# A staging tile for the solve's transposed block, and three engines for the first diagonal copies of the inverse

## The chip, the cores and the metric

The kernel runs on one core of a Trainium2 chip. The metric is the device time of one execution in microseconds (us); lower is better. The kernel before took 1288.86 us as the median of three runs (1288.18 to 1288.86). The five engines are TensorE (PE in the profile), VectorE (DVE), ScalarE (ACT), GpSimd (POOL) and SyncE (SP), which here only issues transfers.

## What is computed

One layer of a two-branch encoder on a 2048 x 1024 float32 input: RMS norm, one input projection, a bidirectional gated delta rule over 4 heads of width 128, a windowed attention over 8 query heads, and one output projection added to the input. The part that matters here is the delta rule. For each head, direction and chunk it needs the inverse of a unit lower triangular matrix:

```python
m = jnp.where(strict, jnp.einsum('bhncd,bhnsd->bhncs', k_beta, k) * decay, 0.0)
t_inv = lax.linalg.triangular_solve(eye + m, jnp.broadcast_to(eye, m.shape),
                                    left_side=True, lower=True, unit_diagonal=True)
...
v_new = u_i - jnp.einsum('bhcd,bhde->bhce', w_i, state)
state = state * jnp.exp(g_last)[..., None, None] + jnp.einsum('bhcd,bhce->bhde', k_dec, v_new)
```

The state runs through all chunks of a head, forward and backward. A head's state steps can't begin before the first inverses of that head exist.

## The kernel before

Phase A (up to about 640 us) does the projections and the attention. Phase B works head by head, `h` = 0 to 3, with 16 chunks of 128 rows in each of two directions. For each head there are four stages:

- `pre_front(h)` loads the keys and queries (tile `kq`, from a ring of two buffers), values and decays four chunks at a time, four times over, and writes the matrices `ma` (line L704). It stores a copy of the key part in DRAM (`m_d`, L709).
- `solve(h)` inverts all 32 x 32 diagonal blocks of the head at once: 128 blocks, one on each partition. The 64 blocks of direction 0 have to be transposed within the partition. They are loaded into the lower half of tile `X` (L732), and DVE copies them, transposed, into `L` (L735). Then POOL clears all of `X` and writes ones on its diagonals (L736, L737). 31 pairs of DVE operations follow (L742 makes `tm`, L746 subtracts it from `X`), and the result goes to DRAM (`x_d`, L747).
- `invert(h)` builds the inverses of the 128 x 128 matrices from the blocks, in four rounds `hi` = 0 to 3. A round loads two groups of blocks (`xc`, L758), transposes them on DVE (`xt`, L759), and copies them onto the diagonals of three matrices `e1`, `e2`, `e3` (named `iv` in the trace; L764, L766, L768: 12 copies on POOL). Five products on PE follow (`pi`, L773), with ACT moving the results (L782 to L797). Each product waits for the one before it.
- `scan(h)` runs the 16 state steps of both directions. `py` (L822) is the matmul in which a step first uses the inverse. Round 0 of `invert` covers chunks 0 to 3 and 12 to 15, with which both directions begin, so the first step waits for round 0 alone.

The source calls `scan(h)`, `pre_front(h+1)`, `solve(h+1)` and `invert(h+1)` in that order, but this is not the order of execution. `set_order` plans the order of all instructions from a table of assumed costs and dependences and fixes it on each engine, so the stages of neighbouring heads overlap. The matmuls of one output projection (`pcs`, L600 to L602) are spread between as independent work. Each engine then works through its own list in order. A change in one place lets the planner lay out the whole program anew.

Of the kernel before, what the change touches and what calls it, by code (L numbers as in the profile page):

```python
# [7 lines left out]
F32 = mybir.dt.float32  # L8
F32R = mybir.dt.float32r
AF = mybir.ActivationFunctionType  # L10
# [5 lines left out]
P = 128  # L16
# [504 lines left out]
def phase_b(ctx, wide, late, tc, t, ident, consts, hp, mix_dn, mix_sw, kq_d, v_d, zdn_d, zsw_d, dp, out):  # L521
    nc = tc.nc
    V, A, G, T = nc.vector, nc.scalar, nc.gpsimd, nc.tensor
    dma = nc.sync.dma_start

    def pool(name, bufs=1, stack=ctx, **kw):
        return stack.enter_context(tc.tile_pool(name=name, bufs=bufs, reuse_waits="tile", **kw))
# [90 lines left out]
    q1 = pool("q1", stack=pre_stack)  # L618
# [6 lines left out]
    quads = [slice(32 * p, 32 * p + 32) for p in range(4)]  # L625
# [100 lines left out]
    def solve(h, H):  # L726
        m_d, x_d, _ = H["solve"]
        L = qa.tile([P, 32, 32], F32, tag="L", name=f"L{h}")
        X = qa.tile([P, 32, 32], F32, tag="X", name=f"X{h}")
        lv = [m_d[d].rearrange("u (p y) -> (u p) y", p=4)[:, : 32 * P] for d in range(2)]  # L730
        lv = [a.rearrange("q (r x) -> q r x", x=P)[:, :, :32] for a in lv]
        dma(X[0:64], lv[0])  # L732
        dma(L[64:128], lv[1])
        x = X.rearrange("p r c -> p (r c)")
        V.tensor_copy(L[0:64], X[0:64].rearrange("p r c -> p c r"))  # L735
        G.memset(x, 0.0)  # L736
        G.memset(x[:, ::33], 1.0)  # L737
        for c in range(31):
            n = 31 - c
            tm = qa.tile([P, 256], F32, tag="tm", name=f"tm{h}_{c}")  # L740
            tv = tm[:, : n * (c + 1)].rearrange("p (r k) -> p r k", k=c + 1)
            V.tensor_tensor(  # L742
                tv, L[:, c + 1 :, c : c + 1].to_broadcast([P, n, c + 1]),
                X[:, c : c + 1, 0 : c + 1].to_broadcast([P, n, c + 1]), ALU.mult,
            )
            V.tensor_tensor(X[:, c + 1 :, 0 : c + 1], X[:, c + 1 :, 0 : c + 1], tv, ALU.subtract)  # L746
        dma(x_d.rearrange("d u (p r) c -> (d u p) (r c)", p=4), X.rearrange("p r c -> p (r c)"))  # L747

    def invert(h, H):
        _, x_d, mp = H["solve"]  # L750
        for hi in range(4):
            e1, p2, e2, e3 = (z[hi % len(z)] for z in zts)
            m = mp[hi]
            x0, x1 = {}, {}
            for d, c4 in ((0, hi), (1, 3 - hi)):
                xc = qb.tile([P, 4, 32], F32, tag="xc", name=f"xc{h}_{d}_{c4}", bufs=4)
                xt = qb.tile([P, 4, 32], F32, tag="xt", name=f"xt{h}_{d}_{c4}", bufs=4)
                dma(xc, x_d[d, 4 * c4 : 4 * c4 + 4].rearrange("u i c -> i u c"))  # L758
                V.transpose(xt.rearrange("p u c -> p (u c)"), xc.rearrange("p u c -> p (u c)"))  # L759
                x0[d], x1[d] = (xc, xt) if d == 0 else (xt, xc)  # L760
            g = qb.tile([P, 4, P], F32, tag="g", name=f"g{h}_{hi}", bufs=2)
            G.tensor_tensor(g, m[:, :, 0], m[:, :, 1], ALU.add)
            for p, q in enumerate(quads):
                G.tensor_copy(e1[q, :, q], x0[p % 2][q])  # L764
            for p, q in enumerate(quads):
                G.tensor_copy(e2[q, :, q], x1[1 - p % 2][q])  # L766
            for p, q in enumerate(quads):
                G.tensor_copy(e3[q, :, q], x0[p // 2][q])  # L768

            def prod(j, lhs, rhs):  # L770
                o = ps_i[(hi + j) % 2].tile([P, 4, P], F32, tag="inv", name=f"pi{j}_{h}_{hi}")
                for c in range(4):
                    T.matmul(o[:, c], lhs(c), rhs(c), start=True, stop=True)  # L773
                return o

            def half(c):
                a = m[:, c].rearrange("p s i -> p (s i)")[:, :384].rearrange("p (e x) -> p e x", x=192)
                return a[:, :, :64]

            o = prod(0, lambda c: g[:, c], lambda c: e1[:, c])  # L780
            b1 = qb.tile([P, 4, P], F32, tag="b1", name=f"b1{h}_{hi}", bufs=2)
            A.activation(b1, o, AF.Copy, scale=-1.0)  # L782
            for d in range(2):
                for q in quads:
                    G.tensor_copy(m[q, :, 1 - d, q], x1[d][q])
            o = prod(1, lambda c: e2[:, c], lambda c: b1[:, c])
            for q, r in ((1, 0), (2, 3)):
                A.activation(e3[quads[q], :, quads[r]], o[quads[q], :, quads[r]], AF.Copy)
            o = prod(2, lambda c: b1[:, c], lambda c: e2[:, c])
            for r, q in ((0, 1), (1, 0), (2, 3), (3, 2)):  # L790
                A.activation(m[quads[r], :, 1 - r % 2, quads[q]], o[quads[r], :, quads[q]], AF.Copy)
            o = prod(3, lambda c: g[:, c], lambda c: e3[:, c])
            for d in range(2):
                A.activation(p2[halves[1 - d], :, halves[d]], o[halves[1 - d], :, halves[d]], AF.Copy, scale=-1.0)
            o = prod(4, lambda c: p2[:, c], half)
            for d in range(2):
                A.activation(m[halves[d], :, 1 - d, halves[1 - d]], o[halves[d], :, halves[1 - d]], AF.Copy)  # L797
# [93 lines left out]
    for f in late:  # L891
        f(zp)
    solve(0, H)
    zts = [[const(f"iv{j}_{i}", [P, 4, P], None, qb) for i in range(2 - j % 2)] for j in range(4)]
    for grp in zts:
        for a in grp:
            G.memset(a, 0.0)
    invert(0, H)
    wide.close()
    with tc.using_default_side("right"):  # L900
# [6 lines left out]
    for h in range(3):  # L907
        scan(h, H)
        H = pre_front(h + 1)
        solve(h + 1, H)  # L910
        invert(h + 1, H)
# [398 lines left out]
```

## Time and profile before

| | before |
|---|---|
| median of 3 runs | 1288.86 us |
| the profiled execution | 1286.12 us, its span 1284.2 us |
| mean granted PE clock in it | 0.993 |
| PE, DVE, ACT, POOL busy | 96%, 70%, 56%, 40% of the span |

The profile is of one execution. The 1.92 us between its time and its span lie outside the recorded instructions. The rows name the line, the engine, the operation and the tile written and read. A bracket at the end tells how long the engine had been idle before the row and what it waited for. A row can stand for several equal instructions (xN); its duration is then theirs together. Times are counted from the start of the span.

### The profile page before, as it was taken

How to read it: one execution, taken by the hardware profiler on the slowest of the kernel's cores; microseconds unless marked ns; L12 is line 12 of the kernel's file. 1: busy time of each engine (PE TensorE's matmuls, PEld its weight loads, DVE VectorE, ACT ScalarE, POOL GpSimd, SP SyncE). 2: the span in 40 equal slices, each digit the busy share in tenths (PEclk: the TensorE clock that was granted, in tenths of full speed). 3: DMA queues.
4: the chain of work that ended last, by engine and by line, in shares of the span. 5: the costliest groups of instructions: out<-in, count | busy, mean ns of one | idle time of the engine just before them, and what ended most of it. 6: DMA issues, size and time to landing. Idle time of an engine off the chain costs nothing.

```text
span 1284.2 us, 22568 instructions
## 1 busy us (share of the span) xinstructions
PE 1227.4 (96%) x7162; PEld 1056.0 (82%) x7162; DVE 901.8 (70%) x2266; ACT 718.8 (56%) x2121; POOL 507.8 (40%) x876
## 2 busy tenths in 40 slices
PE   6999999999999999999999998899799899999998
PEld 6998878788889987888888787788688789898776
DVE  4422488999874679999996583689489779557333
ACT  6421265776644677777665425858557855666210
POOL 2230054566512387774321306513681651641000
PEclk9999999999999999999999999999899999999999
DMA  7442254223544333421237816967965874746765
GB/s 259 150 127 79 97 169 158 88 83 101 177 130 131 121 106 111 124 98 50 75 115 242 237 63 196 283 192 206 278 172 157 242 202 139 207 148 201 242 233 210
DMA packets 225510, 205.35 MB, mean 160 GB/s; under 512 B 48496, under 2 KB 175088, under 8 KB 225392
## 3 DMA queue, kind: packets, MB, share of 16 engines
q1 hardware_dynamic: 225392, 203.92, 51.2%
q8 instruction: 57, 0.93, 0.3%
q14 instruction: 61, 0.50, 0.1%
HBM read 138.79 MB, written 65.08 MB: 159 GB/s over the span
## 4 chain that ended last, share of the span: by engine, by line
PE 67%; DVE 9%; DMA 9%; ACT 5%; POOL 4%; issue 4%; SPq 1%; DVEq 0%; POOLq 0%; ACTq 0%
PE pf_c L190 5%; PE pf_c L191 5%; PE pf_c L192 5%; PE pf_z L190 4%; PE pf_z L191 4%; PE pf_z L192 4%; PE pi L773 3%; PE pt L364 3%; PE pcd L562 2%; PE pcd L563 2%; PE pcd L564 2%; DVE acc L241 2%; PE pcs L601 2%; PE py L822 1%; PE pcs L600 1%
## 5 line engine op out<-in xcount | busy, mean ns | idle before, releaser
L190 PE MATMUL pf_c<-xhi,wh_c 128*128 128x512 f32 x384 | 151.3, 405 | 1.1 <-DVE acc L241 1.1
L191 PE MATMUL pf_c<-xlo,wh_c 128*128 128x512 f32 x384 | 152.0, 404 | 0.0
L192 PE MATMUL pf_c<-xhi,wl_c 128*128 128x512 f32 x384 | 150.6, 404 | 0.0
L241 DVE SCALAR_TENSOR_TENSOR acc<-pf_c,cw,acc 128x512 f32<-128x512 f32 (+1 forms) x192 | 140.4, 742 | 10.4 <-ACT acc L237 8.1
L359 POOL TENSOR_SCALAR pr<-pr,st 128x384 f32<-128x384 f32 (+1 forms) x128 | 88.8, 711 | 72.3 <-DVE st L357 56.5
L190 PE MATMUL pf_z<-xhi,wh_z 128*128 128x512 f32 x256 | 87.0, 403 | 0.5 <-DVE zo L214 0.5
L191 PE MATMUL pf_z<-xlo,wh_z 128*128 128x512 f32 x256 | 86.5, 399 | 0.0
L350 ACT ACTIVATE pr<-pr,st 128x384 f32<-128x384 f32 (+1 forms) x128 | 76.1, 597 | 17.7 <-DVE st L349 16.4
L192 PE MATMUL pf_z<-xhi,wl_z 128*128 128x512 f32 x256 | 85.3, 398 | 0.0
L190 PEld LDWEIGHTS pf_c<-xhi,wh_c 128*128 128x128 f32 x384 | 72.5, 189 | 14.8 <-DVE acc L241 1.5
L192 PEld LDWEIGHTS pf_c<-xhi,wl_c 128*128 128x128 f32 x384 | 72.2, 189 | 13.2
L191 PEld LDWEIGHTS pf_c<-xlo,wh_c 128*128 128x128 f32 x384 | 72.1, 189 | 13.1
L368 ACT ACTIVATE ph<-pt 128x512 fp32r<-128x512 f32 x92 | 53.8, 595 | 41.6 <-PE pt L364 38.2
L345 DVE CUSTOM_DVE_ANT_0 pr<-s,mask,sink 128x384 f32<-128x384 f32 (+1 forms) x128 | 73.0, 592 | 5.7 <-PE pt L364 3.2
L364 PE MATMUL pt<-ident,pr 128*128 128x128 f32 x368 | 72.1, 275 | 3.7 <-DVE pl L369 2.3
L369 DVE TENSOR_TENSOR pl<-pt,ph 128x512 fp32r<-128x512 f32 x92 | 62.0, 682 | 15.7 <-ACT ph L368 14.1
L827 ACT ACTIVATE yk<-py,ck 128x128 f32<-128x128 f32 x120 | 43.9, 366 | 44.6 <-PE py L822 43.3
L364 PEld LDWEIGHTS pt<-ident,pr 128*128 128x128 f32 x368 | 48.0, 140 | 20.2 <-DVE pl L369 4.3
L704 DVE SCALAR_TENSOR_TENSOR ma<-gh,bp,dc 128x256 f32<-128x256 f32 x128 | 54.6, 475 | 11.4 <-PE gh L695 7.6
L600 PE MATMUL pcs<-wohs,mhs 128*128 128x512 f32 x128 | 57.7, 451 | 5.0 <-ACT mhs L594 5.0
L201 PE MATMUL pq_q<-wh_q,xhi 128*128 128x256 f32 x256 | 60.6, 286 | 0.1
L202 PE MATMUL pq_q<-wh_q,xlo 128*128 128x256 f32 x256 | 60.0, 282 | 0.0
(253 smaller groups left out, 3743.7 us busy)
## 6 DMA issues: line engine op xcount, KB each, us to landing
kqc<-kq_d SPq DMA_DIRECT2D x120, 128.0 KB, 2.9
ws_c<-wt SPq DMA_DIRECT2D x48, 256.0 KB, 3.2
xr<-x SPq DMA_DIRECT2D x16, 512.0 KB, 5.5
ws_z<-wt SPq DMA_DIRECT2D x32, 256.0 KB, 3.7
kq<-kq_d SPq DMA_DIRECT2D x16, 512.0 KB, 5.1
m_d<-ma SPq DMA_DIRECT2D x32, 256.0 KB, 5.9
mxs<-mix_sw SPq DMA_DIRECT2D x32, 256.0 KB, 3.3
xrs<-x SPq DMA_DIRECT2D x32, 256.0 KB, 3.5
```

The source lines that it names most:

```text
L190: T.matmul(ps, hi[:, k, cs], xhi[b][:, k], start=(k == 0), stop=False)
L191: T.matmul(ps, hi[:, k, cs], xlo[b][:, k], start=False, stop=False)
L192: T.matmul(ps, lo[:, k, cs], xhi[b][:, k], start=False, stop=(k == KC - 1))
L201: T.matmul(ps[:, :n], xh, hi[:, k, :n], start=(k == 0), stop=False)
L202: T.matmul(ps[:, :n], xl, hi[:, k, :n], start=False, stop=False)
L241: V.scalar_tensor_tensor(av, ps[:, lo:], cw[:, i, k : k + 1], av, ALU.mult, ALU.add)
L345: V.tensor_tensor_reduce(pr[j][:, :n], ps[:, :n], mask[:, lo * P : hi * P], 1.0, sink[:, hh : hh + 1], ALU.add, ALU.max, accum_out=mx[:, j ...
L350: A.activation(pr[j][:, :n], pr[j][:, :n], AF.Exp, bias=nm[:, j : j + 1], accum_out=den[:, j : j + 1])
L359: G.tensor_scalar(pr[j][:, :n], pr[j][:, :n], den[:, j : j + 1], 1.0, ALU.mult, ALU.mult)
L364: T.transpose(pt[:, j], pr[j][:, (kb - lo) * P : (kb - lo + 1) * P], ident)
L369: V.tensor_tensor(pl, ptf, ph.bitcast(F32), ALU.subtract)
L600: T.matmul(ps, mh[:, k], wh[:, k], start=(k == 0), stop=False)
```

## The change

`solve` no longer stages the blocks of direction 0 in `X`. They are loaded into a new tile `lt`, which takes a turn in the ring of two `kq` buffers, and DVE copies them from there into `L`. `X` is cleared without regard to that load. In round 0 of `invert` the four copies for `e1` go to DVE, those for `e2` stay on POOL, and those for `e3` go to ACT. Rounds 1 to 3 keep all 12 on POOL. What is copied, and to where, is as before.

```diff
         X = qa.tile([P, 32, 32], F32, tag="X", name=f"X{h}")
         lv = [m_d[d].rearrange("u (p y) -> (u p) y", p=4)[:, : 32 * P] for d in range(2)]
         lv = [a.rearrange("q (r x) -> q r x", x=P)[:, :, :32] for a in lv]
-        dma(X[0:64], lv[0])
+        lt = q1.tile([P, 2, 512], F32, tag="kq", name=f"lt{h}", bufs=2).rearrange("p a s -> p (a s)")
+        lt = lt.rearrange("p (r c) -> p r c", c=32)
+        dma(lt[0:64], lv[0])
         dma(L[64:128], lv[1])
         x = X.rearrange("p r c -> p (r c)")
-        V.tensor_copy(L[0:64], X[0:64].rearrange("p r c -> p c r"))
         G.memset(x, 0.0)
         G.memset(x[:, ::33], 1.0)
+        V.tensor_copy(L[0:64], lt[0:64].rearrange("p r c -> p c r"))
...
-            for p, q in enumerate(quads):
-                G.tensor_copy(e1[q, :, q], x0[p % 2][q])
-            for p, q in enumerate(quads):
-                G.tensor_copy(e2[q, :, q], x1[1 - p % 2][q])
-            for p, q in enumerate(quads):
-                G.tensor_copy(e3[q, :, q], x0[p // 2][q])
+            for s, a, b in zip("GGG" if hi else "VGA", (e1, e2, e3), ([0, 1, 0, 1], [1, 0, 1, 0], [0, 0, 1, 1])):
+                xs = x1 if a is e2 else x0
+                for q, k in zip(quads, b):
+                    if s == "A":
+                        A.activation(a[q, :, q], xs[k][q], AF.Copy)
+                    else:
+                        (V if s == "V" else G).tensor_copy(a[q, :, q], xs[k][q])
```

Lines of the changed kernel after the first insertion stand two or three higher: L704 and L709 keep their numbers, the copy into `L` is L739, the memsets are L737 and L738, the transposes L761, and the copies L769 (ACT) and L771 (DVE and POOL).

The planner's new order shows at three places around head 1. In tile names the first digit is the head; `xt1_0_0` and `xt1_1_3` are the two transposed groups of its round 0, `iv0_0` is `e1`, `iv2_0` is `e2`.

On DVE, the rows up to round 0 of head 1, before:

```order
L704 TENSOR_SCALAR ma2_0_11666<-gh2_3_0_11779,bp2_11500,dc2_3_1_11744 128x2x128
L704 TENSOR_SCALAR ma2_3_11670<-gh2_3_0_11779,bp2_11500,dc2_3_0_11741 128x2x128
L704 TENSOR_SCALAR ma2_0_11666<-gh2_3_0_11779,bp2_11500,dc2_3_1_11744 128x2x128
L868 TENSOR_SCALAR sso0_0_9854<-sso0_0_9854 128x8
L704 TENSOR_SCALAR ma2_3_11670<-gh2_3_1_11790,bp2_11500,dc2_3_0_11741 128x2x128
L704 TENSOR_SCALAR ma2_0_11666<-gh2_3_1_11790,bp2_11500,dc2_3_1_11744 128x2x128
L704 TENSOR_SCALAR ma2_3_11670<-gh2_3_1_11790,bp2_11500,dc2_3_0_11741 128x2x128
L704 TENSOR_SCALAR ma2_0_11666<-gh2_3_1_11790,bp2_11500,dc2_3_1_11744 128x2x128
L882 TENSOR_SCALAR zt0_0_9883<-tro0_0_9878,dnw_4986,zt0_0_9883 128x512
L759 STREAM_TRANSPOSE xt1_0_0_10521<-xc1_0_0_10520 128x128
```

The same place after:

```order
L704 TENSOR_SCALAR ma2_0_11668<-gh2_0_1_11716,bp2_11502,dc2_0_0_11665 128x2x128
L704 TENSOR_SCALAR ma2_3_11672<-gh2_0_1_11716,bp2_11502,dc2_0_1_11669 128x2x128
L603 TENSOR_TENSOR xrs8_0_11824<-xrs8_0_11824,pcs8_0_11826 128x512
L595 TENSOR_TENSOR mls9_0_11847<-mxs9_0_11841,mhs9_0_11846 128x512
L761 STREAM_TRANSPOSE xt1_0_0_10523<-xc1_0_0_10522 128x128
L771 COPY iv0_0_8892<-xc1_0_0_10522 32x4x32 x2
L704 TENSOR_SCALAR ma2_3_11672<-gh2_3_0_11781,bp2_11502,dc2_3_0_11743 128x2x128
L761 STREAM_TRANSPOSE xt1_1_3_10527<-xc1_1_3_10526 128x128
L871 TENSOR_SCALAR sso0_0_9855<-sso0_0_9855 128x8
L761 STREAM_TRANSPOSE xt1_0_1_10590<-xc1_0_1_10589 128x128
L771 COPY iv0_0_8892<-xt1_1_3_10527 32x4x32 x2
L761 STREAM_TRANSPOSE xt1_1_2_10594<-xc1_1_2_10593 128x128
```

The eight L704 that read `gh2_3`, the last quarter of `pre_front(2)`, stood ahead of round 0 of head 1. Now one stands inside the round and seven behind it. Further up the same list, the last L742 of `solve(1)` has moved from place 1547 to place 1526.

On POOL, the rows up to round 0 of head 1, before:

```order
L869 TENSOR_TENSOR sso0_0_9854<-sso0_0_9854,pw_4992 128x8
L666 TENSOR_TENSOR dc3_1_0_13113<-dc3_1_0_13113,dmask_4984 128x512
L764 COPY iv0_0_8891<-xc1_0_0_10520 32x4x32 x2
L766 COPY iv2_0_8894<-xt1_0_0_10521 32x4x32 x2
L766 COPY iv2_0_8894<-xc1_1_3_10524 32x4x32
L764 COPY iv0_0_8891<-xt1_1_3_10525 32x4x32 x2
```

The same place after:

```order
L685 TENSOR_TENSOR nk2_11501<-ssk2_11500,pw_4992 128x4 x2
L737 MEMSET X2_12026 128x1024
L666 TENSOR_TENSOR dc2_3_0_11743<-dc2_3_0_11743,dmask_4984 128x512
L738 MEMSET X2_12026 128x32
L666 TENSOR_TENSOR dc2_3_1_11746<-dc2_3_1_11746,dmask_4984 128x512
L771 COPY iv2_0_8895<-xc1_1_3_10526 32x4x32 x2
L771 COPY iv2_0_8895<-xt1_0_0_10523 32x4x32 x2
```

The clearing of `X` for head 2 has moved up to here. Two additions of the decay mask for `pre_front(2)` (`dc2_3`), which stood further up before, now stand behind it.

On SP, the first key load of `pre_front(2)` (`kq2_1`), before:

```order
L811 DMA kqc0_0_5_9378<-kq_d0_87 128x2x128
L811 DMA kqc0_1_5_9398<-kq_d0_87 128x2x128
L655 DMA kq2_1_11505<-kq_d2_89 128x2x512
L709 DMA m_d1_9905<-ma1_1_9914 128x4x128
L709 DMA m_d1_9905<-ma1_0_10068 128x4x128
```

The same load after:

```order
L734 DMA lt1_10422<-m_d1_9906 64x32x32
L735 DMA L1_10420<-m_d1_9906 64x32x32
L597 DMA xrs3_0_10309<-x 128x512
L655 DMA kq2_1_11507<-kq_d2_89 128x2x512
L814 DMA kqc0_1_7_9479<-kq_d0_87 128x2x128
L604 DMA part2_7944<-xrs2_0_10286 128x512
L587 DMA mxs4_0_10326<-mix_sw4_75 128x512
L655 DMA kq2_2_11585<-kq_d2_89 128x2x512
```

It stood ahead of the last stores of `m_d1`, which the solve's own load needs; since `lt1` takes its turn in the ring first, it now stands behind the load of `lt1`.

## The prediction

> **What bounds the kernel now.** I read the page first: the busy shares and the chain that ended last.
>
> ```profile
> PE 1227.4 (96%) x7162; PEld 1056.0 (82%) x7162; DVE 901.8 (70%) x2266; ACT 718.8 (56%) x2121; POOL 507.8 (40%) x876
> PE 67%; DVE 9%; DMA 9%; ACT 5%; POOL 4%; issue 4%; SPq 1%; DVEq 0%; POOLq 0%; ACTq 0%
> ```
>
> PE is busy for 1227.4 of 1284.2 us, and the change takes nothing from its work. So it can win only PE idle time, 57 us over the whole span, or time in which PE runs at a lower clock. The question is where that time lies. The first state step of a head is a `py` matmul that reads `vs`; later steps read `r`. The list of PE's instructions shows the last step of head 0 and the first of head 1:
>
> ```profile
> 898.71 0.49 PE L822 MATMUL py<-r,ma 128*128 128x128 f32 x2
> 928.34 0.39 PE L822 MATMUL py<-vs,ma 128*128 128x128 f32 x2
> ```
>
> I cut phase B at such places for all heads and asked for the busy times by stretch. Columns: stretch, length, busy time of PE, its weight loads, DVE, ACT and POOL with the number of instructions, granted clock, share of the DMA engines, GB/s.
>
> ```profile
> 0.00:775.00 775.00, 755.99 (x4176) 644.61 (x4177) 567.47 (x1320) 430.44 (x1038) 314.86 (x480) 1.00 0.41 130
> 775.00:898.70 123.70, 113.64 (x750) 100.15 (x748) 89.60 (x267) 89.48 (x362) 54.84 (x106) 0.99 0.75 217
> 898.70:928.30 29.60, 23.58 (x118) 18.86 (x119) 15.17 (x45) 15.61 (x62) 16.96 (x38) 0.88 0.97 283
> 928.30:1009.80 81.50, 73.06 (x527) 66.11 (x527) 71.29 (x204) 57.64 (x225) 42.25 (x68) 1.00 0.62 180
> 1009.80:1030.20 20.40, 17.25 (x110) 14.56 (x109) 14.30 (x46) 16.49 (x70) 16.61 (x43) 1.00 0.81 236
> 1030.20:1106.50 76.30, 74.44 (x534) 67.47 (x533) 63.81 (x192) 41.27 (x144) 28.90 (x67) 1.00 0.62 183
> 1106.50:1118.30 11.80, 10.34 (x60) 8.87 (x59) 3.99 (x11) 9.25 (x37) 8.96 (x24) 0.86 0.60 168
> 1137.00:1284.20 147.20, 140.41 (x756) 117.63 (x754) 66.51 (x156) 46.83 (x149) 9.45 (x10) 1.00 0.62 209
> ```
>
> The three handovers from head to head last 29.60, 20.40 and 11.80 us. I call them T1, T2 and T3. In each, the old head's steps are done and the new head's wait for its solve and round 0. PE is idle for 6.02, 3.15 and 1.46 us in them. From 1137 us on, the new order of PE's matmuls is the old one, so nothing is won there.
>
> T1 and T3 lose something beside the idle time. The same view in pieces of 4 us:
>
> ```profile
> 906.00:910.00 4.00, 1.51 (x6) 0.68 (x4) 2.85 (x10) 2.22 (x15) 1.14 (x1) 1.00 1.03 318
> 910.00:914.00 4.00, 3.01 (x9) 2.27 (x10) 2.34 (x5) 3.46 (x12) 1.77 (x2) 0.50 0.94 309
> 914.00:918.00 4.00, 3.78 (x13) 2.73 (x12) 0.62 (x2) 0.16 (x1) 2.06 (x8) 0.65 0.90 223
> 1112.00:1116.00 4.00, 2.77 (x15) 2.18 (x15) 1.99 (x5) 2.91 (x9) 3.69 (x6) 0.85 0.26 92
> 1116.00:1120.00 4.00, 4.00 (x23) 3.79 (x23) 1.61 (x3) 2.77 (x10) 3.45 (x12) 0.72 0.67 161
> ```
>
> After a piece with PE busy for 1.51 of 4 us, the granted clock is 0.50 and then 0.65. The loss is 0.50 x 3.01 + 0.35 x 3.78 = 2.8 us in T1, and 0.15 x 2.77 + 0.28 x 4.00 = 1.5 us in T3. So the handovers hold 6.0 + 2.8 + 3.2 + 1.5 + 1.5 = 15 us in all, and T1 has 8.8 of them.
>
> **The start of the solve.** Rows of DVE and POOL around the copy into `L`, for heads 0, 1 and 2:
>
> ```profile
> 735.73 1.12 DVE L735 COPY L<-X 64x1024 f32<-64x1024 f32 x1 [0.63 <-DMA X<-m_d]
> 736.90 0.95 POOL L736 MEMSET X<- 128x1024 f32 x1 [2.79 <-DVE L L735]
> 738.11 0.21 DVE L742 TENSOR_TENSOR tm<-L,X 128x31 f32<-128x31 f32 x1 [1.26 <-POOL X L737]
> 841.60 1.29 POOL L762 TENSOR_TENSOR g<-ma 128x512 f32<-128x512 f32 x1
> 841.77 2.06 DVE L735 COPY L<-X 64x1024 f32<-64x1024 f32 x1
> 845.30 0.20 DVE L742 TENSOR_TENSOR tm<-L,X 128x31 f32<-128x31 f32 x1
> 933.74 2.11 DVE L735 COPY L<-X 64x1024 f32<-64x1024 f32 x1
> 939.00 0.21 DVE L742 TENSOR_TENSOR tm<-L,X 128x31 f32<-128x31 f32 x1 [0.53 <-POOL X L737]
> ```
>
> Before, POOL's clearing stands between DVE's copy and the first step of the solve. In the change it is done ahead, so the first step can follow the copy. DVE's own idle time there is 1.26 us (head 0), nothing (head 1: the row has no bracket, DVE filled the 1.47 us with other rows) and 0.53 us (head 2). That is the direct gain, 0.5 to 1.3 us a head. In head 0 PE has no use for it, since it is full of projections then.
>
> The larger part is the new order. DVE is what a solve has to share with the state steps:
>
> ```profile
> 834.70:905.50 70.80, 67.91 (x456) 59.62 (x455) 63.27 (x204) 51.36 (x213) 18.69 (x20) 1.00 0.71 208
> 1036.40:1092.00 55.60, 54.60 (x402) 50.63 (x401) 49.64 (x149) 30.94 (x104) 15.57 (x35) 1.00 0.55 163
> ```
>
> These are solve 1 and solve 3, from the load of the blocks to the store of the result; DVE is busy for 89% of both. In DVE's list the last L742 of solve 1 moves from place 1547 to 1526, 21 places up. At 63.27 / 204 = 0.31 us an instruction that is up to 6.5 us. Solve 3's last pair moves up 8 places, at 0.33 us each 2.7 us. Solve 2's stays within two. What comes free in T1 is the store and reload, which nothing shortens:
>
> ```profile
> 905.54 7.19 DMA x_d<-X
> 907.44 1.26 DVE L704 SCALAR_TENSOR_TENSOR ma<-gh,bp,dc 128x256 f32<-128x256 f32 x3
> 909.93 1.66 DVE L704 SCALAR_TENSOR_TENSOR ma<-gh,bp,dc 128x256 f32<-128x256 f32 x4 [1.15 <-PE gh L695]
> 915.60 0.66 DVE L759 STREAM_TRANSPOSE xt<-xc 128x128 f32<-128x128 f32 x2 [2.47 <-DMA xc<-x_d]
> ```
>
> From the store at 905.54 to the first transpose at 915.60 are 10.1 us, all inside T1. In the new order some of this trip lies beside the last steps of `scan(0)`. Of the 6.5 us I take 4 as reaching the handover, since PE is busy for 67.91 of 70.80 us in the solve and `scan(0)` can't end earlier by much. Matmuls that filled T1 then run elsewhere, so of 4 us I book **3 us for T1** (bounds: 0, and the whole 8.8). For T3, 8 places give at most 2.7 us, and T3's idle time is 1.46: I book **1 us** (0 to 3.0). For T2, **0.5 us** (0 to 3.15).
>
> **Round 0 on three engines.** Rows of head 1, and the nearest rows for a small copy on DVE and on ACT:
>
> ```profile
> 915.63 0.61 POOL L764 COPY iv<-xc 32x128 f32<-32x128 f32 x2 [3.35 <-DMA xc<-x_d]
> 917.27 0.62 POOL L764 COPY iv<-xt 32x128 f32<-32x128 f32 x2
> 917.94 1.16 PE L773 MATMUL pi<-iv,g 128*128 128x128 f32 x8 [0.22 <-POOL iv L764]
> 931.67 0.48 DVE L838 COPY S<-po 128x128 f32<-128x128 f32 x2
> 921.83 0.56 ACT L788 ACTIVATE iv<-pi 32x128 f32<-32x128 f32 x2 [0.81 <-PE pi L773]
> ```
>
> Before, `e1` is complete at 917.89, 2.3 us after the first copy began, and the first product starts at once. In the change DVE does two transposes (0.66 for the two), four copies (0.24 each by L838), one more transpose and one L704 (about 0.45) before `e1` is complete: about 2.5 us. So the first product starts no earlier, and I book 0 (bounds: 1 us either way). `e3` on ACT costs 4 x 0.28 = 1.1 us a head, and it isn't needed before the fourth product. ACT is busy for half of T1, which covers it; without that cover the 1.1 us would delay the move of the first product. POOL loses 8 copies, 2.4 us a head, but POOL is not what ends last.
>
> Here a rule speaks against the change. The copy into `L` took 1.12 us in head 0, but 2.06 us in head 1, where it began 0.17 us after a POOL row that ended at 842.89 and itself ended 0.94 us after that. The Trainium skill ("SBUF — State Buffer", Who interferes with whom) says that DVE and GpSimd share one pair of SBUF ports under an exclusive lock, and that a DVE copy in a two-port mode makes the other wait for the whole instruction. By that rule, with which those two rows agree, the copies of `e1` and `e2` run one after the other, about 1 us more in each round 0; the sum would be 2 us poorer.
>
> **The ring and the rest.** `lt` costs `kq` its early load:
>
> ```profile
> 813.18 0.52 SPq L655 DMA_DIRECT2D kq<-kq_d  x1
> 864.00 0.27 PE L675 MATMUL tr<-ident,kq 128*128 128x128 f32 x1
> ```
>
> `kq2_1` was loaded at 813.18 and first used at 864.00. In the change it follows `lt1`, whose blocks were loaded at about 835 and copied by 843.83. It still has 20 us, so I book 0. Without that cover, PE's first work of `pre_front` would wait for a load. The first 775 us hold the same work in a slightly different order: 0, with 2 us either way, since no row prices a shuffle.
>
> **Sum:** 3 + 1 + 0.5 = 4.5, less 0.5 for the added DVE and ACT work in the handovers: 4.0 us. The profiled execution would go from 1286.1 to 1282.1; it is 2.7 us below the median of the runs, so the median goes from 1288.9 to **1284.9 us**.
>
> **Rivals.**
>
> *Given back at the second handover (slower).* The L704 at 907.44 and 909.93 ran in the shadow of the store and reload. Seven of those eight now stand behind round 0 of head 1 on DVE. Their decay rows (`dc2_3`) stand on POOL behind the clearing of `X`, which must wait until the store of 7.19 us has read `X`. Their results go to `m_d` and are what solve 2 loads. Round 0's rows would be through 2.5 us after about 911.6 at best, and seven L704 at 0.42 end at about 917, not 911.6: solve 2 starts over 5 us later, while `scan(1)` starts earlier. It decides if DVE can't take these 5 us back within `scan(1)`, where it is busy for 71.29 of 81.50 us. Then T2 grows by 5 us of PE idle time, and if the clock falls as in T1, by 2.8 more: 4.0 won, 7.8 lost, 1292.7 us. For it: DVE's load. Against it: in the new list solve 2 still ends beside the same step of `scan(1)`. Chance 0.27.
>
> *Hidden (no change).* The solve ends earlier, but PE only exchanges one filler for another, and the idle time stays. For it: DVE and PE are both nearly full, and the DMA share in T1 is 0.97. It gives 1288.9. Chance 0.25.
>
> *The clock stays up (faster by more).* If T1 keeps PE busy enough, its 2.8 us and T3's 1.5 us of slow clock go as well: 4.0 + 4.3, so 1280.6. Chance 0.12. The Trainium skill ("TensorE: Matmul & The Clock Gate", Part 1) has a rule that would do this: the clock drops to half after an idle window of about 3.4 us and comes back after a busy one. The rows agree: 0.50 follows a piece that was idle for 2.49 of 4 us.
>
> The forecast has 0.36, at 2.6 to 6 us faster, so 1283 to 1286.3. About 0.2% (2.6 us) is what a measurement here can tell from no change. Faster by more than that is the forecast and the last rival: 0.48. The range reaches from 1279.5 to 1293, which leaves out some of the last rival and the worse half of the slower one.
>
> **What would show it.** Right: the store of `x_d` of head 1 begins before or beside the last step of `scan(0)`; T1 shrinks to about 26 us, with less PE idle time; T2 stays within 1 us of 20.4; `tm` follows the copy into `L` without a wait for POOL. Wrong: T2 grows by as much as T1 shrinks, or the first product of round 0 waits for a copy on DVE or ACT. The forecast falls if PE's idle time between 775 and 1137 us does not go down.

## The result and the profile after

The changed kernel takes 1279.58 us as the median of five runs (1277.23 to 1283.60), against 1288.86 for the kernel before (five runs on the same chip, 1287.14 to 1294.34): ratio 0.9924, 95% interval [0.9905, 0.9944], 9.3 us less. The forecast was 4.0 us less. The profiled execution took 1279.58 us, its span 1277.8; before, 1286.12 and 1284.2. So the two profiled executions differ by 6.5 us, and the other 2.7 are the distance at which the profile of before lay under its median.

The busy shares and the chain that ended last, of the changed kernel:

```profile
PE 1227.3 (96%) x7162; PEld 1057.3 (83%) x7162; DVE 904.5 (71%) x2282; ACT 723.6 (57%) x2137; POOL 502.6 (39%) x844
PE 75%; DVE 9%; ACT 6%; DMA 5%; POOL 2%; issue 2%; SPq 1%; DVEq 0%; ACTq 0%; POOLq 0%
```

PE is busy for as long as before (1227.3 against 1227.4 us). Nearly the whole difference between the two spans, 6.3 of 6.4 us, is PE idle time: 56.8 us before, 50.5 now. The busy times by stretch, cut at the last step of one head and the first of the next; columns as in the prediction:

```profile
0.00:775.00 775.00, 757.03 (x4182) 646.59 (x4183) 570.66 (x1319) 431.17 (x1038) 315.57 (x480) 1.00 0.41 129
775.00:901.70 126.70, 115.16 (x748) 101.01 (x747) 92.86 (x279) 91.43 (x373) 55.11 (x99) 0.97 0.78 220
901.70:926.00 24.30, 20.13 (x104) 17.16 (x103) 14.41 (x42) 14.73 (x54) 16.22 (x39) 0.86 0.94 256
926.00:1010.00 84.00, 77.04 (x550) 68.95 (x548) 70.60 (x217) 59.59 (x233) 42.33 (x68) 1.00 0.73 209
1010.00:1027.00 17.00, 15.30 (x100) 12.85 (x99) 13.03 (x37) 16.30 (x69) 13.45 (x33) 1.00 0.87 231
1027.00:1103.60 76.60, 75.73 (x542) 69.17 (x541) 62.25 (x197) 43.27 (x148) 32.25 (x74) 1.00 0.65 186
1103.60:1113.90 10.30, 9.94 (x73) 8.77 (x72) 4.63 (x12) 7.72 (x33) 8.93 (x21) 1.00 0.73 205
```

The prediction cut T2 of the kernel before two microseconds early, since the last step of `scan(1)` stands at 1011.95. Cut rightly, two rows of before read:

```profile
928.30:1012.00 83.70, 75.26 (x541) 68.02 (x541) 73.49 (x214) 58.87 (x228) 44.20 (x75) 1.00 0.63 182
1012.00:1030.20 18.20, 15.05 (x97) 12.64 (x96) 12.11 (x37) 15.26 (x66) 14.67 (x37) 1.00 0.78 234
```

Length less PE's busy time gives the idle time of each stretch:

| PE idle, us | before | after | difference |
|---|---|---|---|
| up to 775 | 19.0 | 18.0 | -1.0 |
| to the end of `scan(0)` | 10.1 | 11.5 | +1.5 |
| T1 | 6.0 | 4.2 | -1.9 |
| `scan(1)` | 8.4 | 7.0 | -1.5 |
| T2 | 3.1 | 1.7 | -1.4 |
| `scan(2)` | 1.9 | 0.9 | -1.0 |
| T3 | 1.5 | 0.4 | -1.1 |
| the rest | 6.8 | 6.9 | +0.1 |

The handovers hold 4.4 us of the gain, the stretches between and ahead of them 1.9. T1 went from 29.6 to 24.2 us and T3 from 11.8 to 10.2 (the stretches above are rounded to a tenth). Rows around T1, from the list of instructions of the changed kernel:

```profile
899.80 0.45 SPq L749 DMA_DIRECT2D x_d<-X  x1
...
901.74 0.39 PE L825 MATMUL py<-r,ma 128*128 128x128 f32 x2
...
909.73 0.31 DVE L761 STREAM_TRANSPOSE xt<-xc 128x128 f32<-128x128 f32 x1
909.97 0.41 DVE L771 COPY iv<-xc 32x128 f32<-32x128 f32 x2
909.98 0.64 POOL L771 COPY iv<-xc 32x128 f32<-32x128 f32 x2 [1.08 <-DMA xc<-x_d]
...
911.39 0.45 DVE L771 COPY iv<-xt 32x128 f32<-32x128 f32 x2
...
911.99 2.05 PE L776 MATMUL pi<-iv,g 128*128 128x128 f32 x8 [3.40 <-DVE iv L771]
...
925.96 0.38 PE L825 MATMUL py<-vs,ma 128*128 128x128 f32 x2
```

The store of head 1's blocks now begins 1.9 us ahead of the last step of `scan(0)`, where it began 6.8 us behind it. From the store to the first product of round 0 there are 12.2 us, as before (12.4). The trip is not shorter; part of it lies beside work. The clock still falls in T1, which in pieces of 4 us reads:

```profile
908.00:912.00 4.00, 0.60 (x4) 0.22 (x2) 3.14 (x12) 3.93 (x15) 2.72 (x6) 0.90 1.06 266
912.00:916.00 4.00, 4.00 (x15) 3.60 (x16) 1.34 (x4) 2.71 (x9) 3.59 (x10) 0.50 0.76 203
916.00:920.00 4.00, 4.00 (x24) 3.83 (x23) 1.97 (x5) 1.98 (x8) 2.63 (x10) 0.75 1.09 290
```

Here it falls during a wait of PE of 3.40 us. In the kernel before it fell after shorter ones. Of PE's waits in T1 ahead of the fall, the longest is the first of these two; in T3 it is the second:

```profile
908.76 1.13 PE L695 MATMUL gh<-kq 128*128 128x256 f32 x4 [2.38 <-DVE ma L704]
...
1113.76 0.50 PE L600 MATMUL pcs<-wohs,mhs 128*128 128x512 f32 x1 [0.98 <-ACT mhs L594]
```

And the stretch at the end of T3 in which the clock was low (0.50, the third number from the end):

```profile
1114.80:1118.20 3.40, 3.40 (x16) 3.31 (x16) 0.51 (x1) 3.04 (x10) 2.91 (x11) 0.50 0.51 151
```

And the start of the solve in heads 1 and 2, in DVE's list of the changed kernel:

```profile
838.73 1.10 DVE L739 COPY L<-lt 64x1024 f32<-64x1024 f32 x1
...
841.31 0.21 DVE L744 TENSOR_TENSOR tm<-L,X 128x31 f32<-128x31 f32 x1 [1.28 <-DMA L<-m_d]
...
933.29 2.12 DVE L739 COPY L<-lt 64x1024 f32<-64x1024 f32 x1
...
935.80 0.80 DVE L744 TENSOR_TENSOR tm<-L,X 128x31 f32<-128x31 f32 x1
```

In head 2 the wait for POOL (0.53 us before) is gone. Head 1 had none before; now its first step waits 1.28 us for the other half of `L`.

### The profile page after: what moved, and what is told of

Its sections match the earlier page's. It is cut to its first block, busy times and chain, and to the rows that moved or that the text cites. A ratio compares the mean times of both kernels' runs of the same rounds, so it can differ in the third digit from the quotient of the medians.

```text
span 1277.8 us, 22572 instructions
## 1 busy us (share of the span) xinstructions
PE 1227.3 (96%) x7162; PEld 1057.3 (83%) x7162; DVE 904.5 (71%) x2282; ACT 723.6 (57%) x2137; POOL 502.6 (39%) x844
## 4 chain that ended last, share of the span: by engine, by line
PE 75%; DVE 9%; ACT 6%; DMA 5%; POOL 2%; issue 2%; SPq 1%; DVEq 0%; ACTq 0%; POOLq 0%
PE pf_c L190 6%; PE pf_c L191 6%; PE pf_c L192 5%; PE pf_z L190 5%; PE pf_z L191 5%; PE pf_z L192 5%; PE pi L776 4%; PE pt L364 3%; PE pq_q L201 2%; PE pq_q L202 2%; PE pq_q L203 2%; PE pcd L562 2%; PE pcd L563 2%; PE pcd L564 2%; DVE acc L241 2%
## 5 line engine op out<-in xcount | busy, mean ns | idle before, releaser
L241 DVE SCALAR_TENSOR_TENSOR acc<-pf_c,cw,acc 128x512 f32<-128x512 f32 (+1 forms) x192 | 140.6, 742 | 10.1 <-ACT acc L237 8.8
L704 DVE SCALAR_TENSOR_TENSOR ma<-gh,bp,dc 128x256 f32<-128x256 f32 x128 | 55.2, 476 | 16.1 <-PE gh L695 14.0
L818 DVE SCALAR_TENSOR_TENSOR r<-pk,negc,vs 128x128 f32<-128x128 f32 x120 | 41.5, 346 | 26.4 <-PE pk L816 25.7
```

Of the source, the lines that this page charges most:

```text
L241: V.scalar_tensor_tensor(av, ps[:, lo:], cw[:, i, k : k + 1], av, ALU.mult, ALU.add)
L704: V.scalar_tensor_tensor(ma[d, c4][:, c], gh[:, k], bp[:, d, cc : cc + 1], gms[d][:, c : c + 1].to_broadcast([P, 2, P]), ALU.mult, ALU.mult,)
```

## The experiments

A change of code makes the planner lay out everything anew. So the runs ask three things: is the gain the code's or the order's, which half of the code matters, and does the gain survive another order? Ratios are to the kernel before on the same chip.

### Code and order apart

In these kernels the planner first plans one code, and the lists of the other are then sorted by the times of that plan:

```diff
# shortened
-            set_order(tc)
+    times = set_order(tc)        # in a build of the code whose order is wanted
+    set_order(tc, times)         # in the build that runs
```

The old code in the new order:

> The old code (blocks staged in X, all copies on POOL) with every engine's list laid out as the planner laid out the changed kernel; only what the old dependences forbid stands elsewhere (about 40 POOL rows). Theory A, the gain of 9.3 us is in the new order of work: this keeps most of it, 1280 to 1284 us. Theory B, the gain is the waits that the new code removes: nothing is left or the waits cost more in an order not made for them, 1287 to 1292 us.

The new code in the old order:

> The new code (staging tile, round 0 on three engines) with every engine's list as it was before; the 16 first copies each on DVE and ACT stand where they stood on POOL, and one load of keys a head is moved because the ring asks for it. Theory A, the gain is in the new order: 1286 to 1289 us, since only the direct waits of 0.5 to 1.3 us a head are gone. Theory B, the removed waits are the gain: 1280 to 1283 us.

Measured: 0.9969 [0.9955, 0.9983] and 1.0033 [1.0021, 1.0046]. The new order gives the old code 4.0 us, and the new code costs 4.2 us in the old order. The second, 1293.14 us, lies outside what either theory gave. Only the two together give 9.3 us (8.4 when the changed kernel was measured again, below). So the gain belongs neither to the code nor to the order alone.

### One half of the change, planned afresh

```diff
-            for s, a, b in zip("GGG" if hi else "VGA", ...
+            for s, a, b in zip("GGG", ...
```

> The staging tile alone, all 12 copies of round 0 on POOL, planned anew. If the staging tile is what counts (the solve starts and ends earlier): 1279 to 1283 us. If the copies count: 1286 to 1289 us. If any replanning throws the time by some us whatever the edit, it can fall anywhere between 1278 and 1293 us, and the two halves need not add up to the whole.

The other half: the loads and the copy of `solve` as before, the three engines as in the change.

> Round 0 on three engines alone, blocks staged in X as before, planned anew. If the copies count: 1280 to 1284 us. If the staging tile counts: 1286 to 1290 us. If any replanning throws the time by some us: anywhere between 1278 and 1293 us, not the rest of the sum.

Measured: 0.9991 [0.9977, 1.0005] and 0.9999 [0.9984, 1.0013]. Neither half does anything measurable in the order that is planned for it, and the halves don't add up to 9.3 us. Their medians, 1286.96 and 1287.50 us, each lie where the other half was to be the cause; of the three readings only the last, that any replanning throws the time, allows both.

### One half of the change, in a fixed order

Here each half runs in the order of the changed kernel, and the staging tile in that of the kernel before, by the same edit.

> The staging tile alone, with the 12 copies of a first round back on GpSimd; every engine's list follows the changed kernel's. If the staging tile is the half that makes the new order pay (the earlier load and the clearing of X ahead of the copy), about 5 us below the old code in that order: ratio to the kernel before 0.992 to 0.994. If the three engines are that half, it stays where the old code in the new order was, 0.996 to 0.998. If a first round on one engine is a loss in an order that was planned for three, the first product of a round 0 starts over 1 us later than in the changed kernel.

> The three engines alone, with the blocks loaded into X itself as before; every engine's list follows the changed kernel's (8 GpSimd rows, the clearing of X, stand elsewhere). If the staging tile is the half that makes the new order pay, 0.996 to 0.998, as the old code in that order; if the three engines are, 0.992 to 0.994. If each is worth half, both kernels lie near 0.995.

> The staging tile alone, with the 12 copies of a first round on GpSimd, every engine's list after the order of the kernel before, where the whole new code cost 0.0033. If the tile is what costs there (the blocks share the key ring, and in that order a key block's load stands between the solve's two loads), about 1.003. If the three engines cost it (the first copies on VectorE stand behind other rows at the first handover), 0.999 to 1.001, and the solve's first step follows its copy without a wait for GpSimd at no gain.

| | order of before | order of the changed kernel |
|---|---|---|
| old code | 1 | 0.9969 [0.9955, 0.9983] |
| staging tile alone | 1.0027 [1.0012, 1.0043] | 0.9977 [0.9962, 0.9991] |
| three engines alone | not run | 0.9949 [0.9929, 0.9969] |
| both | 1.0033 [1.0021, 1.0046] | 0.9935 [0.9920, 0.9950] |

Against the old code in the same new order, the three engines give 2.6 us (with intervals that overlap) and the staging tile none by itself; both together give 4.4 us. The traces show why the engines count there. With the old code in the new order, POOL's list of round 0 of head 1 reads (line numbers of these kernels are 7 higher):

```profile
909.93 1.41 POOL L778 COPY iv<-xc 32x128 f32<-32x128 f32 x5 [2.17 <-DMA xc<-x_d]
...
911.96 0.95 POOL L778 COPY iv<-xt 32x128 f32<-32x128 f32 x3
912.99 1.65 POOL L879 TENSOR_TENSOR sso<-sso,pw 128x8 f32<-128x8 f32 x1
914.70 0.63 POOL L778 COPY iv<-xt 32x128 f32<-32x128 f32 x2
```

And PE's list, of the same kernel:

```profile
915.04 2.07 PE L783 MATMUL pi<-iv,g 128*128 128x128 f32 x8 [7.10 <-POOL iv L778]
```

A row of another task (`sso`, 1.65 us) stands in the middle of POOL's copies, and the last copy that the first product needs comes behind it. PE waits 7.10 us. The staging tile alone waits 6.71 us at the same place. With the three engines, in the same order:

```profile
903.66 0.89 SPq L756 DMA_DIRECT2D x_d<-X  x1
...
915.50 1.76 PE L783 MATMUL pi<-iv,g 128*128 128x128 f32 x8 [3.45 <-DVE iv L778]
```

From the store to the first product are 11.8 us here, against 15.0 with the old code in this order and 12.4 in its own. So the three engines take away a delay that the new order itself brings. That is a part of how code and order belong together.

In the old order the staging tile costs 3.5 us, most of the 4.2 us that the whole change costs there. SP's list at solve 1, with the staging tile in the old order:

```profile
834.00 0.61 SPq L736 DMA_DIRECT2D lt<-m_d  x1
834.64 3.97 SPq L655 DMA_DIRECT2D kq<-kq_d  x1
838.66 0.61 SPq L737 DMA_DIRECT2D L<-m_d  x1
839.37 3.45 SPq L597 DMA_DIRECT2D xrs<-x  x1
...
844.13 0.38 SPq L587 DMA_DIRECT2D mxs<-mix_sw  x1
```

The kernel before, at the same place:

```profile
834.71 0.61 SPq L732 DMA_DIRECT2D X<-m_d  x1
835.37 3.39 SPq L733 DMA_DIRECT2D L<-m_d  x1
838.79 1.44 SPq L597 DMA_DIRECT2D xrs<-x  x1
...
841.64 0.36 SPq L587 DMA_DIRECT2D mxs<-mix_sw  x1
```

Before, this load of `kq` had been issued 21 us earlier, at 813.18. With `lt` in its ring it can't be, so it stands between the two loads of the solve. One long issue there was usual (`L`, 3.39 us); now there are two, of 3.97 and 3.45 us. The load of `L` itself is hardly later, since its row ended at 838.76 before. But `mxs`, five issues behind `kq`, goes out 2.5 us later. ACT and then DVE wait for it. First the staging tile in the old order:

```profile
848.60 0.63 ACT L594 ACTIVATE mhs<-mxs 128x512 fp32r<-128x512 f32 x1 [4.56 <-DMA mxs<-mix_sw]
...
849.26 0.69 DVE L595 TENSOR_TENSOR mls<-mxs,mhs 128x512 fp32r<-128x512 f32 x1 [3.07 <-ACT mhs L594]
```

Then the kernel before:

```profile
845.54 0.63 ACT L594 ACTIVATE mhs<-mxs 128x512 fp32r<-128x512 f32 x1 [1.40 <-DMA mxs<-mix_sw]
...
846.20 0.69 DVE L595 TENSOR_TENSOR mls<-mxs,mhs 128x512 fp32r<-128x512 f32 x1 [0.70 <-ACT mhs L594]
```

DVE's list has the same order in both kernels, so the solve stands still behind that wait. It goes from its first step to its store in 64.2 us (846.00 to 910.16) instead of 60.2 (845.30 to 905.54). This is one profiled execution of each. DVE waits 3.07 us at that row instead of 0.70, so this wait is 2.4 of the 4.0 us. The state steps stand behind it too: `scan(0)` reaches its last step at 903.19 instead of 898.71. Why the `kq` load held the queue for 3.97 us no row shows.

### The same change in other orders

The planner adds a fixed delay after each instruction, in ns by engine. A step of one in such a delay changes no code and moves as many rows as the change does (1224 to 1528 of PE's):

```diff
-LAG = {"PE": 205, "DVE": 140, "Activation": 160, "Pool": 120, "SP": 2400}
+LAG = {"PE": 205, "DVE": 141, "Activation": 160, "Pool": 120, "SP": 2400}
```

The others differ in the number named. First the changed kernel once more, unedited:

> The changed kernel itself, beside the others on this chip: 0.992 of before, about 1279 us, if the first measurement was right.

> The kernel before, its code untouched; the planner takes 141 ns for DVE's lag where it took 140. That moves 1483 of 6148 rows in PE's list, as many as the change does. Theory lottery (a new layout of the program throws the time by some us, whatever made the planner lay it out): off the 1288 us of before by 2 to 6 us, either way. Theory enabled order (the gain needs the new code): within 2 us of before.

> The changed kernel with DVE's lag taken as 141 ns for 140 by the planner, 1423 rows moved on PE. Theory lottery: the 9 us are not kept, 1282 to 1290 us. Theory enabled order: the new code leads the planner to a good layout however it is nudged, 1277 to 1281 us.

> The kernel before with PE's lag taken as 206 ns for 205 by the planner, 1398 rows moved on PE. Theory lottery: off by 2 to 6 us either way, and not the same as the other nudge. Theory enabled order: within 2 us of before.

> The changed kernel, with the planner's delay after a TensorE instruction at 206 ns for 205; 1528 of TensorE's 6148 rows change place. If the time of this kernel hangs on the order that the planner happens to find, another ratio than 0.9925, in 0.990 to 1.000, and as far from it as the 1 ns step took the kernel before (some 4 us). If the change has a worth of its own, under 0.9965, the figure of the kernel before with the same step. If neither, 0.9925 within 0.0015.

> The kernel before, with the planner's delay after a ScalarE instruction at 161 ns for 160; 1353 of TensorE's 6148 rows change place. If any replanning moves the time by some us, a ratio outside 0.998 to 1.002, of either sign; if the earlier steps of 1 ns were exceptions, 1.000 within 0.0015.

> The changed kernel with the planner's delay after a ScalarE instruction at 161 ns for 160, the pair of the kernel before with this step (0.9985); 1409 of TensorE's 6148 rows change place. If the change is worth its mean over the five pairs so far (0.003), about 0.9955; if it is worth nothing beyond luck, as likely above 0.9985 as below.

> The kernel before, with the planner's delay after a GpSimd instruction at 121 ns for 120; 1224 of TensorE's 6148 rows change place. If an order drawn anew throws the time by some us, a ratio in 0.996 to 1.003 that nothing in the edit foretells; if GpSimd's delay, being the least used engine's, hardly matters, 1.000 within 0.0015.

> The changed kernel with the same step. If the change has a worth of its own under the scatter of the orders, below its pair (the kernel before with this step) by 0.002 to 0.004. If its gain is the one lucky order, no lower than its pair, between 0.996 and 1.004.

> The kernel before, with the planner's delay after a TensorE instruction at 204 ns for 205; 1457 of TensorE's 6148 rows change place. 0.996 to 1.003 if the orders scatter; the step of 1 ns the other way gave 0.9965.

> The changed kernel with the same step; 1476 of TensorE's rows change place. If the change has a worth of its own, below its pair by 0.002 to 0.004; if not, its five orders (0.9925, 0.996, 1.003, and these two) lie as the kernel before's do, around 0.998.

Measured, with the handovers of each profiled execution from the list of state steps (before, then changed; the first row is the original pair of profiles, with the ratio of the repeated run):

| step | ratio, old code | ratio, changed code | difference | T1, us | T2, us | T3, us |
|---|---|---|---|---|---|---|
| none | 1 | 0.9935 [0.9920, 0.9950] | -0.0065 | 29.6, 24.2 | 18.2, 17.0 | 11.8, 10.2 |
| DVE 141 | 1.0011 [0.9994, 1.0028] | 0.9962 [0.9947, 0.9978] | -0.0049 | 36.5, 23.0 | 19.8, 23.7 | 10.9, 8.6 |
| PE 206 | 0.9965 [0.9948, 0.9983] | 1.0033 [1.0019, 1.0047] | +0.0068 | 28.8, 25.6 | 20.2, 20.5 | 11.1, 8.3 |
| ACT 161 | 0.9985 [0.9970, 1.0001] | 0.9972 [0.9954, 0.9990] | -0.0013 | 33.3, 24.5 | 18.6, 21.5 | 10.1, 9.2 |
| POOL 121 | 0.9997 [0.9980, 1.0014] | 0.9923 [0.9901, 0.9945] | -0.0074 | 31.9, 23.5 | 21.3, 19.5 | 10.0, 10.6 |
| PE 204 | 0.9982 [0.9967, 0.9996] | 0.9964 [0.9946, 0.9982] | -0.0018 | 32.7, 28.1 | 18.7, 21.8 | 10.0, 10.6 |
| mean | 0.9990 | 0.9965 | -0.0025 | 32.1, 24.8 | 19.5, 20.7 | 10.7, 9.6 |

A step of 1 ns throws the old code by up to 4.5 us and the changed code by up to 12.6 (from 0.9935 to 1.0033). With the old code, two of the five steps (PE 206 and PE 204) stand clear of 1 with their intervals; those of the other three contain it. The mean difference over six orders is -0.0025, 3.2 us, with a 95% interval of [-0.0080, +0.0029] from the scatter of the six pairs. So by the means about a third of the measured 9.3 us goes with the code, and the rest would be the luck of these two orders: without a step, the old code has the second slowest of its six orders, the changed code the second fastest. The interval is too wide to show that share, since it holds both nothing and the whole of the 9.3 us (a difference of 0.0076 in the ratio).

T1 is another matter. It is shorter with the changed code in all six pairs, and the longest of the changed (28.1) lies under the shortest of the old (28.8). The widest pair, DVE 141, from PE's list of the old code:

```profile
903.98 0.42 PE L822 MATMUL py<-r,ma 128*128 128x128 f32 x2
...
940.53 0.63 PE L822 MATMUL py<-vs,ma 128*128 128x128 f32 x2
```

And of the changed code:

```profile
902.54 0.39 PE L825 MATMUL py<-r,ma 128*128 128x128 f32 x2
...
925.50 0.39 PE L825 MATMUL py<-vs,ma 128*128 128x128 f32 x2
```

The store of `x_d` of head 1 shows the same. Against the last step of `scan(0)` it begins 6.4 to 10.7 us later in the six orders of the old code, and from 3.0 us earlier to 6.2 us later in those of the changed code.

Where do the 7.3 us of T1 go? From the same lists, as means over the six orders: head 0's first step comes 6.2 us later, `scan(0)` is 4.4 us shorter, T1 7.3 shorter, `scan(1)` 2.9 longer, T2 1.2 longer, `scan(2)` and T3 1.0 shorter each, the rest 0.9 shorter. That is, up to rounding, the 4.2 us by which the mean spans differ (1285.3 and 1281.1). Of the 7.3 us, 2.9 are idle time of PE (7.5 and 4.6 us in T1) and 4.4 are busy time of PE: 7 of the 36 `pcs` matmuls of T1 run in `scan(1)` instead, and the mean granted clock in T1 is 0.90 instead of 0.85. With head 0's later start, about 6 us of the 7.3 are made up for by the end of T2. Over the whole span about half of the 4.2 us is idle time of PE and half is busy time: PE is busy for 1227.8 us with the old code and 1225.7 with the changed, for the same matmuls, at a mean granted clock of 0.991 and 0.992. In the one pair that got slower, PE 206, T1 shrank too (28.8 to 25.6). Its loss stands ahead of it: `scan(0)` ends at 906.67 instead of 899.98.

No version beat the changed kernel beyond doubt. With POOL 121 it measures 0.9923, the same within its interval.

## Why the prediction was right or wrong

The direction was right, the size was not: 4.0 us were forecast, 9.3 measured.

- **The failed step** is the sum: beside "the first 775 us hold the same work in a slightly different order: 0, with 2 us either way, since no row prices a shuffle" it had terms for the handovers only, and it carried the distance of 2.7 us between profile and median over to the changed kernel. The first 775 us by themselves gave 1.0 us, within the 2. But all stretches outside the handovers together gave 1.9 us, for which the sum had 0 or no term, and the distance of 2.7 us was 0 in the changed kernel; these two are 4.6 of the 5.3 us that the forecast missed. A shuffle has a price, it applies to the whole program, and it is as large as the change: steps of 1 ns moved the old code by -4.5 to +1.4 us and the changed code by -1.5 to +12.6.
- **The terms of the sum**, in the profiled execution: T1 gave 1.9 us of PE idle time where 3 were booked, T2 1.4 for 0.5, T3 1.1 for 1. Together 4.4 for 4.5, which is partly chance, since one was too large and one too small. The 0.5 us for added DVE and ACT work don't show. The direct gain of 0.5 to 1.3 us a head was no gain in head 1, which had no wait for POOL to lose.
- **The profile and the median**: the sum was carried over from the profiled execution to the median with 2.7 us between them. The changed kernel's profiled execution lies on its median, so 2.7 us more appear in the medians than in the traces, which is luck of the one execution that was profiled: 9.3 = 4.4 + 1.9 + 2.7 + 0.3, where the last is what rounding and the two times outside the spans leave.
- **The mechanism of T1** was right: the store ahead of or beside the last steps (in five of six orders; with PE 204 it begins 6.2 us behind them), T1 near 26 us (24.2, and 23.0 to 28.1 in six orders), no wait for POOL behind the copy into `L`. PE's idle time fell as asked: from 775 us to the end of T3 it went from 31.0 to 25.6 us.
- **Round 0 at 0** was right in size for this kernel (12.2 us from store to product, 12.4 before), but for another reason than given. The sign for "wrong", a first product that waits for a copy on DVE, is there with 3.40 us and means nothing by itself. In the new order the old copies would have come at 15.0 us. Against the rule of the Trainium skill that was weighed there ("SBUF — State Buffer", Who interferes with whom), the copies of `e1` and `e2` began together at 909.97 and 909.98 and took 0.21 and 0.32 us each. POOL alone had taken 0.31 a copy, so no 1 us was lost; whether they ran in the two-port mode of that rule, no row shows. Beside the large copy into `L` (838.73, 1.10 us) the rows do agree with the rule, and there it is POOL that pays:

```profile
838.38 0.29 POOL L771 COPY iv<-xc 32x128 f32<-32x128 f32 x1
838.71 1.28 POOL L771 COPY iv<-xt 32x128 f32<-32x128 f32 x1
```

- **The ring at 0** was wrong as a rule. It looked at whether `kq` comes late and not at what stands behind its load on SP. In the old order the staging tile costs 3.5 us, and a longer wait behind that load is what the trace shows for it. In the new order the two later `kq` loads (837.72 and 840.83) stand behind both loads of the solve (`L` at 834.20).
- **The rivals.** "Given back at the second handover" exists, but small: T2 grew in four of six pairs, by 1.2 us in the mean over all six and 3.9 at most; in the measured pair it shrank, from 18.2 us (20.4 in the prediction, which began it two microseconds early) to 17.0. "The clock stays up" did not come in T1: a granted 0.50 still follows the piece with 0.60 us of work in 4. By the Trainium skill ("TensorE: Matmul & The Clock Gate", Part 1) an idle window of about 3.4 us halves the clock. The wait of 3.40 us fits, but in the kernel before the clock fell with no wait ahead of it longer than 2.38 us in T1 and 0.98 us in T3. So the rows do not agree with the rule as the prediction said, and the measurement decides. In T3 the clock did stay up (1.00, before 0.86); ahead of T1 it was lower than before (0.97 up to the end of `scan(0)`, before 0.99). In the mean over the six pairs, PE's shorter busy time, with a higher clock in T1, is about half of the gain in the traces. The rival that was missing is the shuffle itself.

Not settled: the worth of the change over many orders beyond -0.0025 [-0.0080, +0.0029], and what in an order makes it good. With the code fixed, the orders tried lie up to 14.2 us apart (0.9923 to 1.0033).

## What to carry to other kernels

Where a planner lays out the whole program, compare two codes over several orders, a few of them drawn by steps of 1 ns in the planner's delays, before a gain of under 1% is put down to the code. A handover that shrinks is no gain in itself: ask where the matmuls go that had filled it. When a tile takes a turn in another tile's ring, ask what the displaced load will hold up in the issue queue, not only whether that load is in time. And a sum worked out from one profiled execution gives the next profile, not the next median, until the spread of the runs is known.

## What was not expected of the hardware

An issue on SP can hold the queue for microseconds while its neighbours take 0.3 to 0.6 us: 3.97 us for a `kq` load, and 3.45 for an `xrs` load two places behind it. The executions of one kernel on one core can spread over more than 10 us, so one profile is one draw. The changed kernel with PE 206 ran from 1287.67 to 1299.35 us in 12 runs, and its profiled execution was the fastest of them.
